# Mixer B's low products with v: 66 stationary columns, placed between the next block's transposes

## The chip, the cores and the metric

The kernel runs on one core of one Trainium2 chip. The metric is the device time of one execution in microseconds (us), and less is better. The kernel before was timed three times: 1516.16, 1517.87 and 1518.08 us, median 1517.87 us.

## The reference

The model is a trunk of two layers over 1024 tokens of width 1024, in 32-bit floating point. Layer 0 uses mixer A (attention in a 2-D neighbourhood), layer 1 uses mixer B. Each layer normalises the stream, projects it, mixes, gates the result, projects it back and adds a gated per-layer embedding. The change touches mixer B alone. With 16 query heads of 64 dimensions and 4 key/value heads it computes, after a per-head RMS norm and a rotary turn of q and k:

```
def q_block(qb):
    sc = jnp.einsum('bkgqd,bksd->bkgqs', qb, k).astype(jnp.float32) * scale
    pr = jax.nn.softmax(sc, axis=-1).astype(v.dtype)
    return jnp.einsum('bkgqs,bksd->bkgqd', pr, v)
o = lax.map(q_block, q_blk)            # 128 queries a block
return (o * jax.nn.silu(gate)) @ w_out
```

The second einsum, the product of the softmax weights with v, is what the change rearranges.

## The kernel before

**Splitting.** To keep 32-bit accuracy on fast matmuls, every operand is held as a high part (rounded to the matmul's type fp32r) and a low part (the remainder). The high part is written by ScalarE (ACT), the low part by VectorE (DVE) as a subtraction. The tile V holds, for each of 8 key chunks of 128 keys, 128 columns: columns 0 to 63 are the high part of v, columns 64 to 127 its low part. V is the stationary operand, so one matmul gives 64 rows of output with v's high part and 64 rows with its low part.

**Steps.** Mixer B goes through 128 steps (list `steps` in `mixer_b`). A step is one block of 128 queries of one head, `(h, hf, t)`, with t = 0 to 3; four steps make a group, whose results stand in one accumulation bank, `OP[h, hf]`. A step n consists of

- `f_S`: scores. Four matmuls of 512 columns into a PSUM tile `s`, then DVE's row minimum `mn` (line 1230).
- `f_E`: ACT's exponential into `P` (line 1236).
- `f_T`: eight transposes of 128x128 pieces of P on TensorE (PE, line 1246), four into each of two PSUM tiles `t` (the pool `psT` has two buffers). Each tile is then copied by ACT into `PTh` (line 1248) and subtracted by DVE into `PTl` (line 1249). PTh and PTl hold 256 queries, those of two steps.
- `f_AV`, once for two steps (t = 1 and t = 3): eight matmuls of V with PTh (the high products), then eight of V with PTl (the low products), 256 columns each, all into one half of the bank `OP`. Between the high and the low ones, in one `f_AV` of four, stand the four transposes of `q_stack`, which prepares later queries; these take a tile of the pool psT too.

At t = 1 `f_AV` allocates the bank, tile `o` of the pool `psO`, which has a single buffer. At t = 3 it calls `head_end`, which empties the bank in two pieces: `evac` (ACT, line 530) and `join` (DVE, line 494, 64x512 elements).

**Order.** The order of instructions on each engine is the order in which the program issues them. In `mixer_b` the items of an odd step are issued as: `turn`, transposes of n, exponential of n+1, scores of n+2. Those of an even step: `turn`, products of n-1, exponential of n+1, transposes of n, scores of n+2. `mix` walks through these items and puts pieces of projections (8 to 12 matmuls, "dense") between them, by a running balance of the costs that the items are listed with (`CB`, `CN`); before an odd step's transposes it forces one if none came since the last transposes.

**Posts.** After every item `mix` calls `pulse`, which ticks the list `post`: a job posted with the number k is issued at the k-th pulse from then, and jobs due at the same pulse are issued in the order in which they were posted. `head_end` posts `evac` with 3 (`DO[1]`), and evac posts `join` with 1 (`DY`). `q_stack` posts its first ACT copy with 4 (`QO[0]`), which posts a DVE subtraction (line 1210) with 2 (`DQ`).

```
def evac():
    act.activation(yh, Ops[64:128], AF.Copy, scale=0.5)
    post.add(DY, join)
    norm()
if h == NH - 1 and hf == 1:
    evac()
else:
    post.add(DO[layer], evac)
```

Of the kernel before, what the change touches and what calls it, by code (L numbers as in the profile page):

```python
# [21 lines left out]
NT = 8  # L22
# [9 lines left out]
CB = (1.25, 1.0, 2.0, 0.5, 1.0)  # L32
# [6 lines left out]
FIN = (4, 4)  # L39
# [10 lines left out]
YS = (11, 11)  # L50
YLOAD_A, YLOAD_B = 0, 118
OPEN3 = 5
ULOAD = 5
TAGS_A = [("th", 512, 2), ("tb", 640, 2), None, ("G", 512, 3)]
TAGS_B = [("th", 512, 2)]
# [105 lines left out]
def trunk(ctx, tc, x, wts, rpb, gains, hgains, mask, sides, rope, gain0, out):  # L161
# [118 lines left out]
    def load_y(l, t):  # L280
        for i, (d, src) in enumerate(zip((HTh, HTl), yD[l])):
            k0 = 4 if i and t >= 4 else 0
            (act if t < 4 else sync).dma_start(d[:, t, k0:7].bitcast(F32), src[t, :, k0:7])
# [34 lines left out]
    def mm(ps, a, b, first, last):  # L318
        pe.matmul(ps, a, b, start=first, stop=last, skip_group_check=True)  # L319
# [333 lines left out]
    def mixer_a():  # L653
        jobs = weight_sums()
        with ExitStack() as es:
# [66 lines left out]
            def load_u(h):  # L722
                UT[h] = sb.tile([128, 16, 24], F32, name="u", bufs=1)
                sync.dma_start(UT[h], U2[h].rearrange("p (r c) -> p r c", r=16))
# [249 lines left out]
            for h in range(NH):  # L974
                att = []
                for j in range(NT):
                    n = h * NT + j
                    def head(h=h, j=j):
# [5 lines left out]
                        if h >= 1 and j != 1 and jobs:  # L984
                            jobs.pop(0)()
                        if j == ULOAD and h + 2 < NH:
                            load_u(h + 2)
# [8 lines left out]
                    if h == 15 and j >= YLOAD_A:  # L996
                        for t in ((j - YLOAD_A,) if j < NT - 1 else range(j - YLOAD_A, NT)):
                            att.append((lambda t=t: load_y(0, t), 0.0))
                    if h == 14 and j == OPEN3:
                        att.append((open3, 0.0))  # L1000
# [18 lines left out]
    def mixer_b(pend):  # L1019
        with ExitStack() as es:  # L1020
# [4 lines left out]
            sb = es.enter_context(tc.tile_pool(name="bsb", bufs=2))  # L1025
# [6 lines left out]
            PTl = one.tile([128, NT, 256], F32R, name="PTl")  # L1032
# [10 lines left out]
            gg, ylive = {}, {}  # L1043
            KA, KB, V, QT, QST, P, RS, OP = {}, {}, {}, {}, {}, {}, {}, {}
            later = Later()
            turned = []

            pro = [False, 0]

# [145 lines left out]
            def q_stack(pair, hf):  # L1195
                g = pair // 2
                ps = psT.tile([128, 4, 128], F32, name="t")
                c = slice((pair % 2) * 128, (pair % 2) * 128 + 128)
                for t in range(4):
                    pe.transpose(ps[:, t], QT[g, hf][:, t, c], ident)  # L1200
                raw = sb.tile([128, 512], F32, name="th")
                act.activation(raw, ps.rearrange("p t c -> p (t c)"), AF.Copy)
                for j in range(2):
                    own, oth = slice(64 * j, 64 * j + 64), slice(64 - 64 * j, 128 - 64 * j)
                    qs = sb.tile([128, 512], F32R, name="QS", bufs=3)
                    QST[2 * pair + j, hf] = qs

                    def high(qs=qs, own=own, oth=oth):
                        act.activation(qs[own], raw[own], AF.Copy)
                        post.add(DQ, lambda: dve.tensor_tensor(qs[oth], raw[own], qs[own], ALU.subtract))  # L1210
                    if pro[0]:
                        high()
                    else:
                        post.add(QO[j], high)
# [3 lines left out]
            steps = [(2 * p + j, hf, t) for p in range(8) for hf in range(2) for j in range(2) for t in range(4)]  # L1218

            def f_S(h, hf, t):  # L1220
                g = h // 4
                ps = psS.tile([128, 1024], F32, name="s")
                qt = QST[h, hf][:, t * 128:(t + 1) * 128]
                for kk, kt in enumerate((KA[g], KB[g])):
                    for c in range(2):
                        mm(ps[:, c * 512:(c + 1) * 512], qt, kt[:, c * 512:(c + 1) * 512], kk == 0, kk == 1)
                if t == 0:
                    RS[h, hf] = sb.tile([128, 4], F32, name="rs", bufs=3)
                mn = sb.tile([128, 1], F32, name="mn", bufs=3)
                dve.tensor_reduce(mn, ps, axis=AX.X, op=ALU.min)  # L1230
                P[h, hf, t] = (ps, mn)
# [6 lines left out]

            def f_T(h, hf, t):
                p = P.pop((h, hf, t))  # L1240
                c = slice((t % 2) * 128, (t % 2) * 128 + 128)
                for b in range(2):
                    ps = psT.tile([128, 4, 128], F32, name="t")
                    for i in range(4):
                        k = 4 * b + i
                        pe.transpose(ps[:, i], p[:, k * 128:(k + 1) * 128], ident)  # L1246
                    ks = slice(4 * b, 4 * b + 4)
                    act.activation(PTh[:, ks, c], ps, AF.Copy)  # L1248
                    dve.tensor_tensor(PTl[:, ks, c], ps, PTh[:, ks, c], ALU.subtract)  # L1249
# [4 lines left out]
            def f_AV(h, hf, t):  # L1254
                if t == 1:
                    OP[h, hf] = psO.tile([128, 512], F32, name="o")
                o = OP[h, hf][:, (t - 1) * 128:(t + 1) * 128]
                for k in range(NT):
                    mm(o, V[h // 4][:, k], PTh[:, k], t == 1 and k == 0, False)
                while turned:  # L1260
                    turned.pop(0)()
                for k in range(NT):
                    mm(o, V[h // 4][:, k], PTl[:, k], False, t == 3 and k == NT - 1)
                if t == 3:
                    fin = head_end(sb, h, hf, RS[h, hf], OP.pop((h, hf)), ylive, 1, gg, talloc)
                    if fin:
                        later.add(FIN[1], fin)

            pro[0] = True
            kv, qi = kv_items(0, dve), q_items(0, dve)  # L1270
# [15 lines left out]
            def exps(n):  # L1286
                def f():
                    f_E(*steps[n])
                f.first = True
                return f  # L1290

            def blocks(n):
                def f():
                    f_T(*steps[n])
                f.kind = "apart" if n % 2 else "blocks"
                return f
            for g in range(4):
                att = []
                for n in range(32 * g, 32 * g + 32):
                    h, hf, t = steps[n]  # L1300
                    av = n >= 2 and n % 2 == 0
                    w = CB if av else CN
                    def turn():
                        if WQ.gate:
                            WQ.gate = False
                        later.tick()
                    att.append((turn, w[0]))
                    if av:
                        att.append((lambda n=n: f_AV(*steps[n - 1]), w[1]))
                    te = [(blocks(n), w[2])]  # L1310
                    if n + 1 < len(steps):
                        te.append((exps(n + 1), w[3]))
                    if n % 2 == 0 and n > 0:
                        te.reverse()
                    att += te
                    if n + 2 < len(steps):
                        def scores(n=n):
                            f_S(*steps[n + 2])
                            WQ.gate = n % 2 == 1 if n < 112 else None
                        att.append((scores, w[4]))  # L1320
                    m = n + QS_AT
                    if m % 8 == 0 and m < len(steps):
                        hn, fn, _ = steps[m]
                        att.append((lambda hn=hn, fn=fn: turned.append(lambda: q_stack(hn // 2, fn)), 0.0))
                    if YLOAD_B <= n < YLOAD_B + NT:
                        att.append((lambda t=n - YLOAD_B: load_y(1, t), 0.0))
                if g == 3:
                    att.append((lambda: f_AV(*steps[-1]), CB[1]))
                def gates(p):
                    return [i for hf in range(2) for i in gate_items("bg", p, hf, dalloc, sb, gg)]  # L1330
                dense = []
                if g > 0:
                    dense += left
                if g < 3:
                    qi = q_items(g + 1, pool)
                    kv = kv_items(1, pool) if g == 1 else [None, None]
                    dense += kv[:-2] + qi[:KS] + [k for k in kv[-2:-1] if k] + qi[KS:8] + [k for k in kv[-1:] if k] + gates(2 * g + 1) + qi[8:]
                    left = gates(2 * g + 2)
                else:
                    WQ.cap[3] = 2  # L1340
                    dense += gates(2 * g + 1) + pp_items(1, dalloc, sb, TAGS_B)
                mix(att, dense, hold=HOLD + 1 if g == 3 else 0)
# [456 lines left out]
```

## Time and profile before

| what | us |
|---|---|
| runs | 1516.16, 1517.87, 1518.08 |
| span of the profiled execution, first to last instruction | 1514.0 |
| PE busy in the span | 1483.9 |
| DVE busy in the span | 1087.9 |
| ACT busy in the span | 917.5 |
| mixer B's steps (first transposes to last products) | from 771 to 1328 |

The profile gives the profiled execution's own time as its span of 1514.0 us; the median of the runs is 3.9 us above it, for what lies ahead of the first and behind the last instruction and for the spread between executions. In the profile's rows PE is the matmuls, PEld the loads of the stationary operand, which run beside them. Matmuls are pipelined, so the recorded length of one is longer than the distance from its start to the next one's start; the distance is what a matmul costs. A row of the timeline gives the start, the length, the engine, the line, the operation, the tiles written and read, and how many instructions are merged in it; in brackets stands the idle time of the engine before it and what ended it.

### The profile page before, as it was taken

Reading aid. Unit: us, or ns where it says so; the run is one execution under the profiler, and the core shown is the slowest. Engines: PE = TensorE matmul, PEld = TensorE weight load, DVE = VectorE, ACT = ScalarE, POOL = GpSimd, SP = SyncE. Lnnn points to the kernel's source line nnn. Section 1 sums busy time; section 2 is a strip of 40 time slices with the busy share of each in tenths; the row PEclk is TensorE's granted clock in tenths of the full one; section 3 lists DMA queues with packets and bytes.
Section 4 is the critical chain, followed back from the end, with each engine's and each line's share of the span. In section 5 each row is a group of like instructions: output and inputs, shape, how many; then the busy total and the mean of one; then the engine's idle time right before and its main releaser. Section 6 shows DMA issues by size and latency. Waiting matters only on the chain.

```text
span 1514.0 us, 24782 instructions
## 1 busy us (share of the span) xinstructions
PE 1483.9 (98%) x8880; PEld 1305.0 (86%) x8880; DVE 1087.9 (72%) x2139; ACT 917.5 (61%) x1865; POOL 450.8 (30%) x605
## 2 busy tenths in 40 slices
PE   8999999999999999999999999999999999999997
PEld 8788988988988787888988999989999988888786
DVE  7566476477467499767887786777877887689856
ACT  6667476477477535443467776666767777744432
POOL 1356376387265200010222132453131300000022
PEclk9999999999999999999999999999999999999999
DMA  8235374274122863262210111111101122763123
GB/s 261 94 110 138 70 175 151 64 160 106 36 88 83 321 249 98 84 192 97 76 51 22 33 40 50 46 33 43 58 27 48 38 77 70 236 233 118 60 91 132
DMA packets 91242, 157.43 MB, mean 104 GB/s; under 512 B 18160, under 2 KB 54256, under 8 KB 90608
## 3 DMA queue, kind: packets, MB, share of 16 engines
q1 hardware_dynamic: 85968, 139.86, 28.2%
q0 software_dynamic: 2560, 8.39, 3.7%
q10 hardware_dynamic: 2592, 7.61, 1.5%
q8 instruction: 70, 1.15, 0.3%
q14 instruction: 52, 0.43, 0.1%
HBM read 125.30 MB, written 50.83 MB: 116 GB/s over the span
## 4 chain that ended last, share of the span: by engine, by line
PE 43%; DVE 6%; ACT 2%; issue 1%; DMA 0%; POOL 0%; ACTq 0%; DVEq 0%; POOLq 0%
PE d L319 19%; PE s L319 8%; PE o L319 8%; PE t L1246 7%; PE t L319 1%; DVE xn L1581 1%; DVE PTl L1249 1%; DVE X L1477 0%; DVE mn L1230 0%; PE t L1200 0%; DVE wl L233 0%; DVE HTl L480 0%; DVE HTl L1423 0%; ACT wh L228 0%; ACT P L1236 0%
## 5 line engine op out<-in xcount | busy, mean ns | idle before, releaser
L319 PE MATMUL d<-wh,HTh 128*128 128x256 f32 (+1 forms) x1000 | 332.9, 335 | 2.7 <-ACT HTh L479 1.7
L319 PE MATMUL d<-wh,HTl 128*128 128x256 f32 (+1 forms) x1000 | 328.9, 331 | 0.3 <-DVE HTl L480 0.3
L319 PE MATMUL d<-wl,HTh 128*128 128x256 f32 (+1 forms) x1000 | 327.9, 330 | 0.2 <-DVE wl L1375 0.2
L1249 DVE TENSOR_TENSOR PTl<-t,PTh 128x512 fp32r<-128x512 f32 x256 | 164.6, 684 | 106.3 <-ACT PTh L1248 106.0
L319 PEld LDWEIGHTS d<-wh,HTh 128*128 128x128 f32 x1000 | 188.5, 189 | 22.7 <-ACT HTh L479 2.0
L319 PEld LDWEIGHTS d<-wl,HTh 128*128 128x128 f32 x1000 | 188.5, 189 | 19.7 <-DVE wl L1375 0.6
L319 PEld LDWEIGHTS d<-wh,HTl 128*128 128x128 f32 x1000 | 188.8, 190 | 18.8 <-DVE HTl L480 0.5
L319 PE MATMUL d<-HTh,wh 128*128 128x512 f32 x504 | 204.7, 406 | 0.0
L319 PE MATMUL d<-HTh,wl 128*128 128x512 f32 x504 | 198.0, 393 | 0.0
L319 PE MATMUL d<-HTl,wh 128*128 128x512 f32 x504 | 197.4, 392 | 0.0
L1236 ACT ACTIVATE P<-s,mn 128x1024 f32<-128x1024 f32 x128 | 142.9, 1116 | 47.3 <-DVE mn L1230 46.4
L1248 ACT ACTIVATE PTh<-t 128x512 fp32r<-128x512 f32 x256 | 139.4, 595 | 46.0 <-PE t L1246 45.5
L1230 DVE TENSOR_REDUCE mn<-s 128x1 f32<-128x1024 f32 x128 | 155.0, 1211 | 9.9 <-PE s L319 9.4
L786 POOL TENSOR_TENSOR PTh<-PTh,SIDE 128x256 fp32r<-128x256 f32 x96 | 81.0, 844 | 197.1 <-ACT PTh L781 197.1
L1246 PE MATMUL t<-ident,P 128*128 128x128 f32 x1024 | 134.8, 273 | 2.6 <-DVE PTl L1249 2.0
L319 PE MATMUL s<-KA,QS 128*128 128x512 f32 (+2 forms) x384 | 134.2, 404 | 2.8 <-DVE mn L760 2.8
L1246 PEld LDWEIGHTS t<-ident,P 128*128 128x128 f32 x1024 | 115.5, 140 | 12.8 <-DVE PTl L1249 6.9
L319 PE MATMUL s<-KB,QS 128*128 128x512 f32 (+2 forms) x384 | 121.4, 370 | 0.0
L319 PE MATMUL o<-PTl,V 128*128 128x256 f32 (+2 forms) x672 | 120.1, 290 | 1.1 <-DVE PTl L1249 0.6
L233 DVE TENSOR_TENSOR wl<-wstage,wh 128x1024 fp32r<-128x1024 f32 x78 | 98.1, 1259 | 31.6 <-ACT wh L228 31.3
L319 PE MATMUL o<-PTh,V 128*128 128x256 f32 (+2 forms) x672 | 118.4, 287 | 2.4 <-POOL PTh L786 1.1
L319 PEld LDWEIGHTS d<-HTh,wl 128*128 128x128 f32 x504 | 94.6, 188 | 21.7
(247 smaller groups left out, 2891.8 us busy)
## 6 DMA issues: line engine op xcount, KB each, us to landing
wstage<-in_wts SPq DMA_DIRECT2D x88, 512.0 KB
pp<-ppD SPq DMA_DIRECT2D x32, 256.0 KB
X<-in_x SPq DMA_DIRECT2D x15, 512.0 KB
rb<-rD SPq DMA_DIRECT2D x56, 128.0 KB
ppD<-th SPq DMA_DIRECT2D x20, 256.0 KB
tD0t<-in_wts SPq DMA_DIRECT2D x16, 256.0 KB
tD1t<-in_wts SPq DMA_DIRECT2D x16, 256.0 KB
xD<-X SPq DMA_DIRECT2D x8, 512.0 KB
```

The lines of the kernel that those rows point to most:

```text
L233: eng.tensor_tensor(lo[:, c:c + n], s[:, c:c + n], hi[:, c:c + n], ALU.subtract)
L319: pe.matmul(ps, a, b, start=first, stop=last, skip_group_check=True)
L786: pool.tensor_tensor(pt[:, 3 * j - 1:3 * j + 4:4], pt[:, f1:f1 + 1].to_broadcast([128, 2, 128]), SIDE[:, :2], ALU.mult)
L1230: dve.tensor_reduce(mn, ps, axis=AX.X, op=ALU.min)
L1236: act.activation(p, ps, AF.Exp, bias=mn, scale=-1.0, accum_out=RS[h, hf][:, t:t + 1])
L1246: pe.transpose(ps[:, i], p[:, k * 128:(k + 1) * 128], ident)
L1248: act.activation(PTh[:, ks, c], ps, AF.Copy)
L1249: dve.tensor_tensor(PTl[:, ks, c], ps, PTh[:, ks, c], ALU.subtract)
L1581: dve.scalar_tensor_tensor(xn, X[t], rn[m][:, i:i + 1], g1, op0=ALU.mult, op1=ALU.mult)
```

## The change

The low products leave `f_AV`. It now issues the eight high products (and `q_stack`'s transposes) alone, and leaves a list of eight functions in `lows`, one per key chunk. The next `f_T`, that of the even step in which the `f_AV` stands, takes the list and issues one low product after each of its eight transposes. The last `f_AV`, which has no transposes behind it, issues its low products itself.

Each low product uses columns 0 to 65 of V in place of all 128 (`NARROW = 66`), and writes 66 rows of the bank in place of 128. What falls away is the product of the low part of P with the low part of v, but for its first two columns; with the small PTl it is of second order.

`head_end` for a group moves with the last low product of t = 3, from the item of the products into the item of the transposes, two items later in the same step.

```
+NARROW = 66
...
+            lows = []
...
             def f_T(h, hf, t):
                 p = P.pop((h, hf, t))
+                low = lows.pop(0) if lows else []
                 c = slice((t % 2) * 128, (t % 2) * 128 + 128)
                 for b in range(2):
                     ps = psT.tile([128, 4, 128], F32, name="t")
                     for i in range(4):
                         k = 4 * b + i
                         pe.transpose(ps[:, i], p[:, k * 128:(k + 1) * 128], ident)
+                        if low:
+                            low.pop(0)()
...
                 while turned:
                     turned.pop(0)()
-                for k in range(NT):
-                    mm(o, V[h // 4][:, k], PTl[:, k], False, t == 3 and k == NT - 1)
-                if t == 3:
-                    fin = head_end(sb, h, hf, RS[h, hf], OP.pop((h, hf)), ylive, 1, gg, talloc)
-                    if fin:
-                        later.add(FIN[1], fin)
+
+                def low(k):
+                    mm(o[:NARROW], V[h // 4][:, k, :NARROW], PTl[:, k], False, t == 3 and k == NT - 1)
+                    if t == 3 and k == NT - 1:
+                        fin = head_end(sb, h, hf, RS[h, hf], OP.pop((h, hf)), ylive, 1, gg, talloc)
+                        if fin:
+                            later.add(FIN[1], fin)
+                lows.append([lambda k=k: low(k) for k in range(NT)])
...
                 if g == 3:
-                    att.append((lambda: f_AV(*steps[-1]), CB[1]))
+                    def end():
+                        f_AV(*steps[-1])
+                        for f in lows.pop():
+                            f()
+                    att.append((end, CB[1]))
```

## The prediction

> **What bounds the kernel now.** I read the page first, then a table of mixer B's stretches, then the timeline of single steps. In the table stand, for each stretch, its length and the busy time (and number) of PE, PEld, DVE, ACT and POOL.
>
> ```profile
> span 1514.0 us, 24782 instructions
> ...
> PE 1483.9 (98%) x8880; PEld 1305.0 (86%) x8880; DVE 1087.9 (72%) x2139; ACT 917.5 (61%) x1865; POOL 450.8 (30%) x605
> ...
> 769.00:900.00 131.00, 130.67 (x922) 119.08 (x922) 102.67 (x162) 97.82 (x180) 30.46 (x44) 1.00 0.10 31
> 900.00:1210.00 310.00, 308.64 (x2178) 285.38 (x2177) 233.00 (x382) 217.22 (x415) 102.33 (x166) 1.00 0.15 44
> 1210.00:1331.00 121.00, 117.41 (x734) 102.15 (x733) 90.57 (x126) 88.88 (x158) 6.22 (x4) 1.00 0.38 123
> ```
>
> In mixer B's steps (769 to 1331 us) PE is idle for 131.00 - 130.67 + 310.00 - 308.64 + 121.00 - 117.41 = 5.3 us of 562; DVE stands at 76% and ACT at 72%. So PE's own stream sets the end: whatever shortens it is gained, and every new wait of PE is lost, nearly one for one.
>
> **What the pairs gain.** How fast PE goes through one step is in the distances of this piece, of an even step:
>
> ```profile
> 906.13 1.12 PE L319 MATMUL o<-PTl,V 128*128 128x256 f32 x8
> 907.10 1.03 PE L1246 MATMUL t<-ident,P 128*128 128x128 f32 x8
> 907.89 0.47 PE L319 MATMUL d<-HTh,wh 128*128 128x512 f32 x1
> 908.20 0.39 PE L319 MATMUL d<-HTl,wh 128*128 128x512 f32 x1
> 908.43 0.40 PE L319 MATMUL d<-HTh,wl 128*128 128x512 f32 x1
> ```
>
> Eight low products take 907.10 - 906.13 = 0.97 us, 120 ns each. From the first transpose to the second d are 1.10 us; one d of 512 columns takes 908.43 - 908.20 = 0.23, so eight transposes take 0.87, 109 ns each. There is no charge for passing from products to transposes or back in these sums. Why does a transpose, with 128 moving columns, cost nearly as much as a product with 256? Mixer A has two products with 128 moving columns:
>
> ```profile
> 515.25 0.19 PEld L319 LDWEIGHTS o<-PTl,V 128*128 128x128 f32 x1
> 515.36 0.19 PEld L319 LDWEIGHTS d<-wh,KA 128*128 128x128 f32 x1
> 515.47 0.19 PEld L319 LDWEIGHTS d<-wl,KA 128*128 128x128 f32 x1
> ...
> 515.25 0.22 PE L319 MATMUL o<-PTh,V 128*128 128x128 f32 x1
> 515.30 0.27 PE L319 MATMUL o<-PTl,V 128*128 128x128 f32 x1
> ```
>
> The second is issued 0.05 to 0.06 us after the first (58 ns before rounding: what 128 moving columns cost), but the loads follow each other at 0.11 us and hold the stream. So 110 ns is the pace of loading 128 stationary columns. The transposes, at 109, go at the pace of their loads, and the array idles half the time; a product with 256 columns (120) hides the next load. In the new order a transpose is followed by a low product whose load has 66 columns. No row shows a narrow load. Above, it is bounded by the full 110: then transpose and product cost 110 + 120 = 230 and nothing is gained. Below, by nothing: then the transpose's own 58 remains. In proportion, 66/128 of 110 is 57, which is hidden behind the 58, so the lower end and the proportional price agree, and I take 58 + 120 = 178 ns a pair. Eight pairs take 1.42 us in place of 0.97 + 0.87 = 1.84, a gain of 0.42 us in each of 63 even steps (2 to 126): **-26 us**; the ends are 0 and -26.
>
> The Trainium skill ("TensorE: Matmul & The Clock Gate") has rules for either end. Its section "LDWEIGHTS (loading the stationary operand)" puts a load at the number of columns over 1.2 per ns: 107 ns for 128, which the trace's 110 bears out, and, as an estimate, 55 for 66. The table at its head says of the stationary operand "128×128 (always)", which would speak against any gain from narrowing it. By the first the term is -26, by the second 0; no run here shows which.
>
> **What moves with it: the bank's release.** `head_end` now runs in the transposes' item. Counting pulses: before, it ran at the products of an even step, and its three pulses were products, exponential, transposes; so evac came behind the transposes, and join one pulse later, behind the scores. Now the three are transposes, scores, and the next step's turn; join comes behind the next, odd step's transposes, on DVE *behind both PTl subtractions* of it. The bank has one buffer, so the first high product of the next group (t = 1, in the next even step) must wait for join. That wait is in the trace already, where join came late:
>
> ```profile
> 1265.58 0.68 DVE L494 SCALAR_TENSOR_TENSOR Y<-o,Y 64x512 f32<-64x512 f32 x1
> ...
> 1266.41 1.19 PE L319 MATMUL o<-PTh,V 128*128 128x256 f32 x8 [0.31 <-DVE Y L494]
> ```
>
> Join takes 0.68 us, and the product starts 0.14 after its end. Behind the waiting product stands all of PE's stream. How late will join be? In steps 4 to 6:
>
> ```profile
> 790.92 0.67 DVE L494 SCALAR_TENSOR_TENSOR Y<-o,Y 64x512 f32<-64x512 f32 x1
> 791.55 1.29 DVE L1249 TENSOR_TENSOR PTl<-t,PTh 128x512 fp32r<-128x512 f32 x2
> 792.87 0.69 DVE L1210 TENSOR_TENSOR QS<-th,QS 64x512 fp32r<-64x512 f32 x1
> ...
> 792.09 1.11 PE L319 MATMUL o<-PTh,V 128*128 128x256 f32 x8
> ```
>
> Join stood at 790.92 and was free early. Now it comes behind the PTl pair (to 792.84) and, in every other group, behind `q_stack`'s QS as well, which is due at the same pulse and was posted one pulse earlier. Join then runs from 793.59 to 794.27 and the products start at 794.41 in place of 792.09: 2.3 us. Three more places, each with the product that would wait:
>
> ```profile
> 807.51 1.29 DVE L1249 TENSOR_TENSOR PTl<-t,PTh 128x512 fp32r<-128x512 f32 x2 [0.31 <-ACT PTh L1248]
> ...
> 807.76 1.11 PE L319 MATMUL o<-PTh,V 128*128 128x256 f32 x8
> ```
>
> ```profile
> 924.52 0.69 DVE L1210 TENSOR_TENSOR QS<-th,QS 64x512 fp32r<-64x512 f32 x1
> ...
> 925.17 1.12 PE L319 MATMUL o<-PTh,V 128*128 128x256 f32 x8
> ```
>
> ```profile
> 942.83 1.29 DVE L1249 TENSOR_TENSOR PTl<-t,PTh 128x512 fp32r<-128x512 f32 x2 [0.25 <-ACT PTh L1248]
> ...
> 944.78 1.12 PE L319 MATMUL o<-PTh,V 128*128 128x256 f32 x8
> ```
>
> Without QS at 807: 808.80 + 0.03 + 0.68 + 0.14 - 807.76 = 1.9. From about 900 us a projection piece (1.4 us) stands between transposes and products and covers most of it: with QS 925.21 + 0.85 - 925.17 = 0.9, without 944.12 + 0.85 - 944.78 = 0.2. I did this sum at each of the 31 places. Without the piece: five with QS at 2.3 (11.5 us) and three without at 1.8 (5.3). With the piece: eight with QS at 1.0 on average (8.3) and nine without at 0.33 (2.9; the largest where join's old place had delayed PTl and that relief is counted). Three with more projections in between: 0.6 together. The one at 1266: 1.9 net of the waits it has now. The last two, where `load_y` items add a pulse that brings join ahead of PTl: 0. Sum **+30.5 us**. The bounds: if another DVE job due at that pulse stands before join too (I estimate 0.4 us at six to eight places), up to 34; if DVE's order shifts in my favour by QS's 0.69 at half of the thirteen places that have it and wait, 26, and I go down to 24.
>
> **Smaller terms.** In 13 groups `q_stack`'s transposes stand right ahead of an even step's transposes, whose second tile needs the buffer that ACT must copy first:
>
> ```profile
> 785.67 0.60 PE L1200 MATMUL t<-ident,qt 128*128 128x128 f32 x4
> 786.02 1.20 PE L319 MATMUL o<-PTl,V 128*128 128x256 f32 x8
> ...
> 786.30 0.60 ACT L1202 ACTIVATE th<-t 128x512 f32<-128x512 f32 x1 [0.56 <-PE t L1200]
> ```
>
> The copy ends at 786.90. The low products were its cover (0.97 us); now PE reaches that tile at 786.02 + 4 pairs = 786.73 and waits till about 787.0: 0.2 to 0.3 each, **+3 us** (0 to 5). The even transposes come 0.97 us earlier towards the exponential they read; where that could get tight, the wait for join has already given the time back, so I cost it at nothing (without that cover at most 0.97 us a place). Of PE's 5.3 us of idle time, about **-1.5** goes with the earlier PTl. The other engines do the same work. Sum: -26 + 30.5 + 3 - 1.5 = **+6 us**, to the profiled 1514.0 as to the median 1517.87 (3.9 above it): **1524 us**.
>
> **The rivals.** (1) *The join is no wait*: it comes ahead of PTl, or PE arrives later than my sums have it. It decides from a mean wait of 0.8 us a group (26/31): under that the change is faster. For it speaks that DVE has 24% to spare; against it the order of issue, in which nothing lets join pass PTl, and the row at 1266.41. With no wait: 1517.9 - 26 + 3 - 1.5 = 1493; with half of it 1508. (2) *The change doesn't do what it says*: a 66-column load takes as long as one of 128, or alternating costs what the boundaries above don't show. The gain is 0, the wait stays: 1517.9 + 30.5 + 3 - 1.5 = 1550. For it speaks only that no narrow load is in the trace. (3) *They cancel*: the forecast's terms with the waits at their low bound of 24: 1517.9 - 26 + 24 + 3 - 1.5 = 1517, no change.
>
> **How the numbers follow.** Forecast, with its own range of 1514 to 1534 and rival 3 inside it: 0.64, of which slower 0.48, no change 0.13, faster 0.03. Rival 1, from 1490 to 1513: 0.22, of which faster 0.19, no change 0.03. Rival 2: 0.14, slower. A measurement of this kernel can't tell less than 0.2% (3 us) from no change. Faster 0.22, same 0.16, slower 0.62. The range from 1502 to 1545 leaves out the far part of rival 1 and most of rival 2, about 2 in 10.
>
> **What would show it.** Right: loads of the low products about 57 ns after a transpose's, eight pairs in 1.4 us; PE idle at the t = 1 products with join (Y) as the releaser, 25 us or more in sum, over 2 us each before 900 us; join behind two PTl on DVE. Wrong: pairs at 230 ns (rival 2); join ahead of PTl, or idle time under 20 us there (rival 1); a third wait of over 5 us that I haven't named.

## The result and the profile after

The changed kernel takes 1557.02 us (median of four runs, 1555.51 to 1558.72) against 1517.01 for the kernel before (four runs, 1515.46 to 1518.08). The ratio is 1.0265, with a 95% interval from 1.0251 to 1.028: 40 us slower, where 7 had been forecast and 28 was the upper end of the range. The profiled execution has a span of 1554.8 us, 40.8 more than before.

First the page, with the engines' busy time, share and instructions:

```profile
span 1554.8 us, 24830 instructions
...
PE 1494.4 (96%) x8880; PEld 1310.3 (84%) x8880; DVE 1095.2 (70%) x2139; ACT 919.0 (59%) x1865; POOL 448.7 (29%) x605
```

Then mixer B's stretch in the table of windows (length; busy time of PE, PEld, DVE, ACT, POOL; granted clock, of which 1.00 is full speed; DMA share; GB/s). It now ends about 40 us later, so it is taken to 1371:

```profile
769.00:1371.00 602.00, 566.30 (x3823) 512.19 (x3822) 430.43 (x666) 404.76 (x751) 136.53 (x214) 0.98 0.17 53
```

The same number of PE instructions (x8880 in the whole kernel) leaves PE idle for 602.00 - 566.30 = 35.7 us, where it was 5.3: 30.4 more. And PE is busy for longer: 566.30 in place of 130.67 + 308.64 + 117.41 = 556.72, 9.6 more, at a mean clock of 0.98 in place of 1.00. Idle and busy time together are the stretch, so they add up to the 40 us whatever their causes. So two questions: what are the 9.6 us, and where is the forecast gain of 26?

The idle time first. PE's groups in mixer B (busy time, mean ns of one; then the idle time just before them and what ended it), the high products of the kernel before ahead of three groups of the changed one, and the changed kernel's waits of PE (total, times, longest):

```profile
L319 PE MATMUL o<-PTh,V 128*128 128x256 f32 x512 | 72.0, 283 | 1.2 <-DVE Y L494 0.8 <-ACT PTh L1248 0.3
...
L1249 PE MATMUL t<-ident,P 128*128 128x128 f32 x1024 | 190.0, 276 | 1.3 <-ACT th L1137 0.9 <-ACT P L1238 0.3 <-DVE PTl L1254 0.2
L320 PE MATMUL o<-PTl,V 128*66 128x256 f32 x512 | 129.6, 371 | 0.0
L320 PE MATMUL o<-PTh,V 128*128 128x256 f32 x512 | 74.7, 289 | 31.9 <-DVE Y L495 24.0 <-ACT rb L572 5.9 <-ACT th L618 1.2
```

```profile
PE o L320 <- DVE Y L495: 24.0, 19, 2.3
PE o L320 <- ACT rb L572: 5.9, 4, 2.2
```

Of the 35.7 us, 31.9 stand ahead of the high products, with join (Y) as the main releaser; 2.4 more are a wait of another user of the bank (o, L514), for join as well. Where the profile names ACT (rb, th), the product waits for join too: at 28 of the 31 t = 1 products, these among them, it starts 0.15 us after join's end. One place on DVE and on PE:

```profile
790.92 1.29 DVE L1254 TENSOR_TENSOR PTl<-t,PTh 128x512 fp32r<-128x512 f32 x2 [0.53 <-ACT PTh L1253]
792.24 0.69 DVE L1212 TENSOR_TENSOR QS<-th,QS 64x512 fp32r<-64x512 f32 x1
792.94 0.68 DVE L495 SCALAR_TENSOR_TENSOR Y<-o,Y 64x512 f32<-64x512 f32 x1
```

```profile
793.77 1.54 PE L320 MATMUL o<-PTh,V 128*128 128x256 f32 x8 [2.15 <-DVE Y L495]
795.11 0.41 PE L1249 MATMUL t<-ident,P 128*128 128x128 f32 x1
795.18 0.56 PE L320 MATMUL o<-PTl,V 128*66 128x256 f32 x1
795.54 0.41 PE L1249 MATMUL t<-ident,P 128*128 128x128 f32 x1
```

Join stands behind two PTl and QS, ends at 793.62, and the product starts 0.15 later, behind 2.15 us of idle time. That is the wait as forecast.

The pairs next. At a place where nothing disturbs them:

```profile
814.07 0.27 PE L1249 MATMUL t<-ident,P 128*128 128x128 f32 x1
814.10 0.36 PE L320 MATMUL o<-PTl,V 128*66 128x256 f32 x1
814.30 0.27 PE L1249 MATMUL t<-ident,P 128*128 128x128 f32 x1
814.33 0.36 PE L320 MATMUL o<-PTl,V 128*66 128x256 f32 x1
814.53 0.27 PE L1249 MATMUL t<-ident,P 128*128 128x128 f32 x1
```

From transpose to transpose a pair takes 0.23 us (228 ns over a block), 0.03 of it to the start of the product and 0.20 from there on. Eight pairs are 1.82 us, where the two blocks apart had cost 1.84. Over 63 steps that is about 1 us; the gain of 26 isn't there.

Last, PE at 795.11 above: there a pair takes 0.43. The table of windows, cut at the edges of the clock's steps (length, busy PE and instructions, granted clock, DMA share, GB/s), shows why:

```profile
790.99:794.40 3.41, 1.26 (x8) 1.00 0.00 0
794.40:797.82 3.42, 3.42 (x19) 0.50 0.02 5
828.54:831.95 3.41, 1.38 (x12) 1.00 0.12 34
831.95:835.36 3.41, 3.41 (x17) 0.50 0.42 120
...
1210.83:1214.24 3.41, 1.39 (x12) 1.00 0.22 64
1214.24:1217.66 3.42, 3.42 (x17) 0.50 0.32 90
...
845.60:849.02 3.42, 1.91 (x13) 1.00 0.00 0
849.02:852.43 3.41, 3.41 (x27) 1.00 0.01 1
```

Six times in mixer B (at 794.4, 831.9, 903.6, 1214.2, 1303.0 and 1340.5 us) the granted clock is 0.50 for 3.41 us, each time behind a long wait for join. Before, there was no such window in mixer B. A window at half clock loses at most half its length: 6 x 3.41 / 2 = 10.2 us. What was done in the six windows takes 9.4 us more, from start to start, than the same kinds of matmul take outside of them (pairs: 0.43 for 0.23).

### The profile page after: what moved, and what is told of

The parts are those of the page before. It is cut to its first block, busy times and chain, and to the rows that moved or that the text cites. A ratio compares the mean times of both kernels' runs of the same rounds, so it can differ in the third digit from the quotient of the medians.

```text
span 1554.8 us, 24830 instructions
## 1 busy us (share of the span) xinstructions
PE 1494.4 (96%) x8880; PEld 1310.3 (84%) x8880; DVE 1095.2 (70%) x2139; ACT 919.0 (59%) x1865; POOL 448.7 (29%) x605
## 5 line engine op out<-in xcount | busy, mean ns | idle before, releaser
L1249 PE MATMUL t<-ident,P 128*128 128x128 f32 x1024 | 190.0, 276 | 1.3 <-ACT th L1137 0.9
L320 PE MATMUL o<-PTl,V 128*66 128x256 f32 (+3 forms) x672 | 176.4, 355 | 0.5 <-POOL PTl L787 0.2
L1249 PEld LDWEIGHTS t<-ident,P 128*128 128x128 f32 x1024 | 132.6, 142 | 8.5 <-ACT th L1137 1.1
L320 PEld LDWEIGHTS o<-PTh,V 128*128 128x128 f32 x672 | 97.7, 191 | 47.3 <-ACT P L1238 28.9
L234 DVE TENSOR_TENSOR wl<-wstage,wh 128x1024 fp32r<-128x1024 f32 x78 | 97.6, 1253 | 31.9 <-ACT wh L229 31.3
```

Of the source, the lines that this page charges most:

```text
L234: eng.tensor_tensor(lo[:, c:c + n], s[:, c:c + n], hi[:, c:c + n], ALU.subtract)
```

## The experiments

Three questions were put to the chip: whether the late join alone makes the loss; why the pairs gain nothing (the narrow load is as slow as a wide one, or it is short and nothing waits for it); and whether the half-clock windows cost what the sum leaves over.

**The new order, with join early.** The changed kernel, with evac posted two pulses earlier, so that join comes ahead of the next transposes' PTl:

```
-DO = (2, 3)
+DO = (2, 1)
```

> The changed kernel with head_end's delay cut from 3 pulses to 1 (DO[1]): evac and join are issued where they stood before the change, while the low products stay narrow and between the transposes. Theory (the loss is the wait for join, 31 us in the changed kernel's trace, and the half-speed clock windows that follow the longest of these waits, some 8 us; the pairs themselves gain nothing, 228 ns against 109 + 120): all of the loss goes, 1515 to 1521 us, pairs still at 228 ns, idle at the t = 1 products under 2 us. Rival (alternating transposes and products is itself what costs): 1535 us or more. Forecast's first term (-26 us) had it been right: 1491 to 1497.

It took 1517.05 us (ten runs, 1516.19 to 1520.72) against 1517.12; ratio 1.0006, interval 0.9996 to 1.0015. Mixer B's window and the largest of PE's waits:

```profile
769.00:1331.00 562.00, 554.92 (x3831) 505.55 (x3829) 428.01 (x667) 403.00 (x751) 139.03 (x216) 1.00 0.19 58
```

```profile
PE t L1249 <- ACT P L1238: 4.6, 8, 0.8
```

The waits for join are gone (0.4 us are left at the t = 1 products), the clock stays at 1.00, and the whole loss of 40 us with them. What remains is the new order of low products and transposes by itself, and it is worth nothing: pairs stay at 228 ns, as in the changed kernel. With the wait gone the even transposes do reach the exponential too early, at eight places, by 0.8 us at most; PE's idle time is 562.00 - 554.92 = 7.1 us, 1.8 more than before.

**The old order, with join late.** The kernel before, low products wide and in a block, with evac posted two pulses later:

```
-DO = (2, 3)
+DO = (2, 5)
```

> The kernel before with the delay raised from 3 pulses to 5 (DO[1]): low products as before, 128 columns and in f_AV; only evac and join are issued as late as in the changed kernel. Theory (wait and clock windows are the whole loss): 1550 to 1558 us, waits for join of about 31 us in sum, five or six half-speed windows of 3.4 us. Rival (the alternation is part of the loss): 1520 to 1545 us.

It took 1560.19 us (1558.65 to 1560.98); ratio 1.0288, interval 1.0269 to 1.0306. PE's waits, and four rows of its windows at the edges of the clock's steps:

```profile
PE o L319 <- DVE Y L494: 24.5, 19, 2.6
PE o L319 <- ACT rb L571: 5.9, 4, 2.1
```

```profile
901.00:904.42 3.42, 1.39 (x12) 1.00 0.13 36
904.42:907.83 3.41, 3.41 (x19) 0.50 0.44 123
...
829.32:832.74 3.42, 1.66 (x14) 1.00 0.20 57
832.74:836.15 3.41, 3.41 (x23) 1.00 0.34 97
```

The same waits, again six windows at half clock, and a little more than the whole loss, without any of the change's new order. The two runs together are a table of two by two: join early, 1517 in either order; join late, 1557 in the new and 1560 in the old.

**One pulse.** The changed kernel with evac one pulse earlier, in place of two:

```
-DO = (2, 3)
+DO = (2, 2)
```

> The changed kernel with head_end's delay at 2 pulses in place of 3: join is then issued at the next step's turn, one pulse earlier, which puts it on DVE ahead of that step's two PTl subtractions. Theory (the loss hangs on whether join stands behind or ahead of PTl in DVE's queue): the whole loss goes with this one pulse, 1515 to 1521 us, idle at the t = 1 products under 3 us in sum. Rival (the loss grows with the delay): about midway, 1530 to 1540 us.

It took 1517.93 us (ten runs, 1514.73 to 1519.19) against 1517.41; ratio 1.0000, interval 0.9991 to 1.0009. The groups show where PE idles:

```profile
L1249 PE MATMUL t<-ident,P 128*128 128x128 f32 x1024 | 186.2, 273 | 5.6 <-ACT P L1238 4.5 <-ACT th L1137 0.9 <-DVE PTl L1254 0.2
...
L320 PE MATMUL o<-PTh,V 128*128 128x256 f32 x512 | 72.0, 283 | 2.6 <-DVE Y L495 1.3 <-ACT rb L517 1.0 <-ACT PTh L1253 0.3
```

Idle time ahead of the high products falls from 31.9 to 2.6 us. The loss hangs on one pulse: whether join is issued ahead of the odd step's PTl or behind it.

**What sets the pace of a transpose and of a narrow product.** The kernel before, with streams of 24 matmuls each put behind mixer B's last step; their results are used by nothing. The streams follow each other on PE, and most differ in one thing from a neighbour (some of them, each loop written on one line; `go(out, stationary, moving)` is a matmul with v's tile as the stationary operand, `w` is a 128x128 piece of PTh read as 32-bit data, `wr` the same as fp32r and `idr` the identity as fp32r):

```
+for i in range(24): go(ps[:66, :128], v[:, i % NT, :66], PTh[:, i % NT, :128])
+for i in range(24): pe.transpose(ps[:, :128], w, ident)
+for i in range(24): pe.transpose(ps[:66, :128], w[:, :66], ident)
+for i in range(24): pe.transpose(ps[:, :66], w[:66], ident[:66, :66])
+for i in range(24):
+    pe.transpose(ps[:, :128], w, ident)
+    go(ps[:66, 128:256], v[:, i % NT, :66], PTh[:, i % NT, :128])
...
+for i in range(24): pe.transpose(ps[:, :128].bitcast(F32R), wr, idr)
+for i in range(24): go(ps[:, :128], v[:, i % NT], PTh[:, i % NT, :128])
```

> The kernel before with streams of 24 matmuls each added behind mixer B's last step, for their pace alone (their results are used by nothing; the time is longer by them). Three theories for the pair that stays at 228 ns. L (a load of 66 columns takes as long as one of 128): 66 stationary x 128 moving goes at 110 ns like 128 x 128; transposes with 66 stationary columns at 109. M (a 32-bit transpose occupies the array for its own 109 ns, loads don't set its pace): 66 x 128 goes at 58 to 60; transposes with 66 stationary columns stay at 109; transposes with 66 moving columns fall under 109, if their load allows; a transpose with a narrow product of 128 columns takes 109 + 58 = 167 or, if the transpose's load is long, 218. S (switching costs): transposes with 66 stationary columns and narrow products are both fast alone, and slow only in alternation. [...]

The run took 1549.8 us (one execution; it is longer by the streams). In the timeline of PE, the columns behind the tiles are the stationary operand and the moving one:

```profile
1335.26 1.42 PE L1353 MATMUL t<-PTh,V 128*66 128x128 f32 x21
...
1339.44 2.78 PE L1361 MATMUL t<-ident,PTh 128*128 128x128 f32 x24
1342.06 2.78 PE L1363 MATMUL t<-ident,PTh 128*66 128x128 f32 x24
1344.68 1.66 PE L1365 MATMUL t<-ident,PTh 66*128 66x66 f32 x24
1346.18 0.28 PE L1367 MATMUL t<-ident,PTh 128*128 128x128 f32 x1
...
1351.63 0.27 PE L1370 MATMUL t<-ident,PTh 128*128 128x128 f32 x1
1351.65 0.30 PE L1353 MATMUL t<-PTh,V 128*66 128x128 f32 x1
1351.79 0.28 PE L1370 MATMUL t<-ident,PTh 128*128 128x128 f32 x1
1351.83 0.30 PE L1353 MATMUL t<-PTh,V 128*66 128x128 f32 x1
...
1360.46 2.23 PE L1376 MATMUL t<-PTl,PTh 128*128 128x128 f32 x24
1362.53 2.86 PE L1353 MATMUL t<-PTh,V 128*128 128x128 f32 x24
```

```profile
L1353 PE MATMUL t<-PTh,V 128*66 128x128 f32 x21 | 1.4, 221 | 0.0
```

- *A narrow load is short.* 21 products with 66 stationary and 128 moving columns take 1.42 us, of which the last one's recorded length is 0.22: 20 distances in 1.20, 60 ns. With 128 stationary columns (1362.53) it is (2.86 - 0.28) / 23 = 112. So the load for 66 columns takes 60 ns at most.
- *A transpose isn't paced by its load.* 24 of them take 1342.06 - 1339.44 = 2.62 us, 109 ns; with 66 stationary columns in place of 128, 1344.68 - 1342.06 = 2.62, the same. With 66 moving columns (and 66 rows) they take 1346.18 - 1344.68 = 1.50, 62.5 ns, and load 128 columns each in that time. So the pace goes with the moving operand: 109 / 128 = 0.85 ns a column, 62.5 / 66 = 0.95. Whether it goes by its columns or by its rows wasn't separated.
- *Behind each other they add.* A transpose and a product of 66 by 128 take 0.16 to 0.18 in the rows (172 ns over the stream): 109 + 63. With 256 moving columns the pair takes 227: 109 + 118, what the changed kernel's pairs take. A transpose with a product of 128 by 128 columns takes 195, less than 109 + 112: beside a transpose the wide load is hidden in part.

In the changed kernel, then, the narrow load did become shorter, and nothing had been waiting for it. In the stream at 1360.46 the transposes have operands of the type fp32r; they take (1362.53 - 1360.46) / 24 = 86 ns. Why 86 wasn't looked into, and using it for P would drop P's low part.

**Filled waits.** If the half clock comes of PE's idling, work that has no use but keeps PE busy in the waits should give the clock back. The changed kernel, with six more score matmuls of 512 columns (1.39 us) ahead of the scores in the steps before the eleven longest waits; the scores overwrite them:

```
+FILL = {(5, 9, 13, 17, 21, 25, 29, 77, 93, 101, 113)[i] + 2 for i in range(11)}
...
+if steps.index((h, hf, t)) in FILL:
+    for _ in range(6):
+        mm(ps[:, :512], qt, KA[g][:, :512], True, True)
```

> The changed kernel with six matmuls of 512 columns (1.39 us) added in front of the scores that stand ahead of each of the eleven longest waits for join (over 1.5 us in the changed kernel's trace); their result is overwritten by the scores. Join is due at the same time, so the added work only fills the wait. Theory (an idle stretch of about 2 us can put TensorE to half clock for a window of 3.41 us, and six such windows in mixer B cost about 1.3 us each): the windows go, the waits fall by 15 us and the added work takes 15 us, so the time falls by 6 to 9 us, to 1548 to 1551 us although PE has more to do. Rival (the windows cost nothing, or have another cause): 1556 us or more, 1572 if the added work isn't hidden.

It took 1549.89 us (1549.04 to 1553.78) against 1517.41; ratio 1.0219, interval 1.02 to 1.0238. PE's waits, and the window that was 602 us for the changed kernel:

```profile
PE o L320 <- DVE Y L495: 12.0, 19, 1.4
```

```profile
769.00:1371.00 602.00, 581.65 (x3924) 523.97 (x3924) 434.94 (x673) 408.14 (x756) 137.07 (x214) 1.00 0.18 56
```

PE does 11 x 1.39 = 15.3 us more work, which takes the place of as much waiting (16.5 us of idle time are left ahead of the high products, of 31.9), and the kernel is 1557.0 - 1549.9 = 7 us faster. One window at half clock is left in mixer B in place of six. Five windows for 7 us is 1.4 us each, under the bound of 1.7; since the two kernels ran in different groups of runs, each with a spread of 3 to 5 us, that size is good to about a half.

## Why the prediction was wrong

The direction was right and the time was not: 1557 is outside 1502 to 1545, and the change lost 40 us where +6 had been summed.

**The pairs, -26: wrong, measured about -1.** The step that failed is "The transposes, at 109, go at the pace of their loads, and the array idles half the time". The 109 ns of a transpose and the 110 ns of a 128-column load are equal by chance. The load's 110 came from mixer A's products, where it holds; it was carried over to the transposes because the number fitted, and because a product of that many columns took 58. The streams show that a transpose takes 109 ns whether its load has 128 columns or 66. So in both orders transposes and products went at their own pace, 109 + 117 to 120, and a shorter load had no gap to shorten. In the groups of the kernel before, every transpose has 128 columns on both sides; two of them:

```profile
L1246 PE MATMUL t<-ident,P 128*128 128x128 f32 x1024 | 134.8, 273 | 2.6 <-DVE PTl L1249 2.0 <-ACT th L1135 0.5
...
L1200 PE MATMUL t<-ident,qt 128*128 128x128 f32 x64 | 10.0, 274 | 0.6 <-POOL qt L1098 0.6
```

So these rows couldn't tell a transpose that waits for its load from one that takes 109 ns itself, and the end of 0 should have had as much weight as -26.

Both rules of the Trainium skill ("TensorE: Matmul & The Clock Gate") had been put beside this term. The one in the section "LDWEIGHTS (loading the stationary operand)", a load in proportion to its columns (estimated from it: 55 ns for 66), agrees with the streams (60 ns at most), and the "128×128 (always)" of the table at its head does not, as far as the load's time goes. The term took the first rule rightly and was still wrong, since neither rule says what a transpose waits for.

**The wait for join, +30.5: right in kind, some 5 low in size.** PE's idle time ahead of the high products grew by 31.9 - 1.2 = 30.7 us. But the forecast had counted from start to start, and there each wait is 0.16 us longer than its idle time, since the recorded end of the matmul ahead covers that much: 2.15 us in the rows are 2.3 in starts, as forecast. In starts the high products lost 34.6 us and L514 1.6, together over the upper bound of 34. The eight places without a projection piece came as forecast (15.8 us of idle time, 17 in starts, for 16.8). At four others a reduction (DVE, L1079, 0.4 us) stands ahead of join, as the upper bound had allowed for, and PE idles 1.37 or 2.10 us. At L514, one of the two places put at 0, join did come ahead of PTl, but behind a subtraction of a weight (L234, 1.2 us). Join stands behind the two PTl and, in every other group, behind QS. Both runs with join early, and the one with join late in the old order, show that this one pulse carries the loss.

**The clock: not in the sum, about 9 us.** The prediction quoted windows whose clock was 1.00 and didn't ask what new idle time of 2 us would do to it. "A third wait of over 5 us" had been named as what would make it wrong; what came isn't a wait, but slower work behind the waits. Counted in starts over the same 3800 matmuls of mixer B, from the first transpose to the last low product, the changed kernel takes 41.7 us more: 36.2 of waits for the bank (34.6 and 1.6, as above), 9.4 of half clock, less 2.4 of other waits and less 1.4 for all the rest, the new order among it.

**The smaller terms.** `q_stack`'s second tile, +3: measured 0.9 (the row of the transposes, th L1137). With pairs at 228 in place of 178 ns the four pairs cover the copy almost to its end, so the term went with the failed one. The exponential, at nothing: 0.3 us in the changed kernel, because the wait for join gives the time back; with join early 4.6 us at eight places, 0.8 at most, inside the bound of 0.97 that was set for lost cover. PE's other idle time, -1.5: the 2.4 above, so about right.

**The rivals.** The second, "The change doesn't do what it says", had nearly the right amounts, gain 0 and the wait in full, and its 1550 is what came but for most of the clock's loss. Of its two reasons the first is refuted (60 ns, not 112), and the second isn't needed: alternating costs nothing (228 ns a pair, against 109 + 120). Its chance of 0.14 was too low, because the end "nothing is gained" had been tied to a slow load alone; a load that nobody waits for is a third way to it. The first rival fell (31.9 us of waits), and so did the third.

## What to carry to other kernels

That two durations are equal is no sign that one causes the other: before a stream's pace is put down to its loads, look for a row in which the load changes and the pace doesn't, or measure streams that differ in the stationary columns alone and in the moving columns alone. Where a single buffer is released by a job in a counted queue, moving the job's origin by one item can put it behind a longer job; count its place again, and move the count with it (here one pulse in `DO` is worth 40 us). New idle time of PE is to be costed with the clock that it loses, not by its length alone.

## What the runs showed of the hardware that was not expected

**The clock falls after less idle time than the length of its window.** In mixer B all the half-clock windows of a run are 3.41 us long and lie on one grid: from 794.40 to 831.95 are 37.55 us, 11 lengths of 3.413; from 903.63 to 1214.24 are 310.61, 91 lengths. The Trainium skill ("TensorE: Matmul & The Clock Gate", the section on the clock gate, Part 1) gives a window of 3413 ns that runs freely, and the trace agrees with it. It says that the clock is halved after an idle window, and the trace differs: PE's idle time inside one window of the grid counts, and part of the window is enough. In mixer B of the changed kernel and of the one with join late in the old order, all twelve windows with 2.02 us of idle time or more (3.41 - 1.39 at 1210.83) are followed by one at half clock, and none of the others, of which the largest has 1.76 (3.42 - 1.66 at 829.32). So there the edge lies between 1.76 and 2.02 of 3.41 us, and the same wait costs the clock or not by where it falls on the grid. Of the nine waits of over 2.02 us in the changed kernel six cost it. The other three straddle an edge, and each window counts only its part, as with the wait of 2.17 us that ends at 867.06 (1.19 and 0.98 us of idle time, clock unchanged):

```profile
862.67:866.08 3.41, 2.22 (x16) 1.00 0.00 0
866.08:869.50 3.42, 2.44 (x22) 1.00 0.02 5
```

The recorded idle time isn't the whole condition, though. In the first 16 us of an execution less is enough: in the kernel before, 3.42 - 1.63 = 1.79 us,

```profile
8.62:12.04 3.42, 1.63 (x12) 1.00 1.03 420
12.04:15.45 3.41, 3.12 (x14) 0.50 1.02 416
```

and 1.59 with join late in the old order (at 6.71 us). In the run with one pulse, 1.91 us at 51.93 are not followed by half clock. What else counts stays open.

**A 32-bit transpose with 128 moving columns takes 109 ns, whether its load has 66 columns or 128.** That is 0.85 ns for each moving column, nearly twice the 117 / 256 = 0.46 of an fp32r product.

**A product of 66 stationary and 128 moving columns takes 60 ns, one of 128 by 128 takes 112.** The 112 are not the time of every load of 128 columns: those of the transposes follow each other at 62.5 ns (66 rows, 32-bit) and at 86 (fp32r). So a narrower stationary operand can pay in a stream of products with 128 moving columns (60 for 112), less between transposes (172 for 195 a pair), and not with 256 (117 to 120 either way).
